# Half-size fetch and late split of three w_out row blocks, an earlier fetch of the second token tile, and other yields in the last head

## The chip, the cores and the metric

The kernel runs on one core of one Trainium2 chip. The metric is the device time of one execution in microseconds (us), the median of several runs. Before the change it is 2442.86 us (three runs, 2440.97 to 2443.92).

## The reference

One layer of a hybrid diffusion backbone over 2048 latent tokens of width 1024, with a context prefix of 256 tokens. Cut to what matters here:

```python
h = modulate(rmsnorm(x, norm_mix[l]), sh1, sc1)
o, _, _ = token_mixers(h @ w_in[l], ...)      # gated recurrence (4 heads) and spatial gating (4 heads)
x = x + g1 * (o @ w_out[l])                   # output projection, gated residual
h2 = modulate(rmsnorm(x, norm_ffn[l]), sh2, sc2)
x = x + g2 * conv_ffn(h2, w_up[l], conv_w[l], conv_b[l], w_down[l], rows)
return rmsnorm(x, norm_final)
```

Everything is float32. `w_out` has 1024 rows (eight blocks of 128, called k = 0 to 7) and 1024 columns (two halves of 512, called n = 0 and 1).

## The kernel before, in words

**Arithmetic.** A large product is made from three fp32r matmuls of 128x512 (`mm3`): each operand is split in a high part, made by a cast on ScalarE (ACT), and a low part, made by a subtraction, here on VectorE (DVE). The helper `split` (L133 and L134) issues both. The product is hi·hi + hi·lo + lo·hi.

**Stages.** The first stage (up to about 973 us of the profile) does the input projections (`pj`), the recurrence heads (`hg`, `deferred`) and the spatial gating heads (`sgu`). Its results go to DRAM as `oT`, one array for each half of the tokens. The second stage multiplies `oT` by `w_out`: 16 token tiles of 128 tokens, for each of them two column halves times eight row blocks times three matmuls, so 48 matmuls into a PSUM tile `dn`. The third stage is the up projection (tiles `Ah`, `Al`, results `ux`, `uz`) with the convolution, the fourth the down projection (`thl`, `mhl`).

**Order of the work.** The projections of the first stage run through `run_banks`, and between their matmuls two queues of side work are stepped: `hg_q` (heads) and `bg_q` (weights). A step is a Python generator that yields a number: it is the time in the program's own count of TensorE work that must pass before the next step is issued. `drain()` steps a queue to its end without regard to these numbers; `gates_done()` issues all pending output gates at once. A scheduler then orders the instructions of each engine; those wrapped in `pin` keep their program order. All DMAs are issued from one queue, that of SyncE (SP), in order: a DMA that must wait holds up those behind it.

**w_out.** `w_out_ops` (about 375 to 538 us) loads each of the 16 pieces (128 rows, 512 columns), multiplies it by the gate, splits it in `hi` and `lo` and stores both halves (512 KB) to `wo_d`. Blocks k = 0 to 2 are fetched back during the last recurrence head (`wo_early`, L916).

**The border.** Ahead of the last four projection banks (`wo_hook`, `seq[len(seq) - 4]`) `open_wo` runs: `hg_q.drain()`, `gates_done()`, `bg_q.drain()`, and then it closes the heads' SBUF pool and opens the pool `pw` in its place. Its generator `load` issues the fetch of the first token tile (`raw<-oT`, L1138) and ten fetches of 512 KB (`wo<-wo_d`, L1144: k = 3 to 7, for n = 0, then for n = 1), and after a yield of 17.0 splits the first tile into `o`. After the first stage's end the second stage's loop issues the fetch of the second token tile (`raw<-oT`, L1316, into a tile of the next pool), then the fetch of the residual rows (`raw<-in_x_dram`, L1326); at the head of iteration t the tile t+1 is split by `split_o`. The last two spatial gating products are made by GpSimd (POOL, L685) and stored by L686 (`oT<-nt`), on the same SP queue. The result of a tile is read by DVE (L1357) and squared by ACT (L1359).

**Placement.** Tiles with `align_bytes=AL` start at a multiple of 512 bytes in their partition; the others start wherever the packer puts them. Of the fp32r matmul operands the four of the heads' column sums (`kh`, `kl`, `knh`, `knl`) and `ones_r` have no such request; the others have.

Of the kernel before, what the change touches and what calls it, by code (L numbers as in the profile page):

```python
# [9 lines left out]
F32 = mybir.dt.float32  # L10
F32R = mybir.dt.float32r
# [7 lines left out]
P = 128  # L19
D = 1024  # L20
NK = D // P
# [5 lines left out]
NH = 4  # L27
# [4 lines left out]
EPS = 1e-6  # L32
LV = [1, 2, 4, 8, 16, 32, 64]
AL = 512

# [46 lines left out]
def tile_trunk(ctx, tc, x, c, cx, c_ctx, w_ada, b_ada, norm_mix, norm_ffn, w_in, hg_norm, sgu_g, sgu_b,  # L84
               w_sp, b_sp, w_out, w_up, conv_w, conv_b, w_down, norm_final, masks, out):
    nc = tc.nc
    V, S, G, T = nc.vector, nc.scalar, nc.gpsimd, Tensor(nc.tensor)
    ld = nc.sync.dma_start
    st = nc.sync.dma_start
    pin = tc.keep_in_program_order  # L90
# [25 lines left out]
    oT_d = [dr.tile([P, NK, TH], F32, name=f"oT{hh}") for hh in range(2)]  # L116
# [14 lines left out]
    def split(hi, lo, raw, eng=None, keep=lambda i: i):  # L131

        keep(S.copy(hi, raw))  # L133
        (eng or G).tensor_sub(lo, raw, hi.bitcast(F32))  # L134
# [48 lines left out]
    hg_q, bg_q = Pump(), Pump()  # L183
# [7 lines left out]
    with es1:  # L191
# [536 lines left out]
        def gate_later(hh, h, g0, on, r, sg):  # L728
            at = {"key": (hh, h), "to": (hh, h, g0, on, sg), "r": r}
            gates.append(at)  # L730
            hg_q.later(lambda: o_scale(at), 4.0)
            hg_q.later(lambda: gate_now(at), 7.5)

        def o_scale(at):
            r, on = at.pop("r", None), at["to"][3]
# [4 lines left out]
        def gate_now(at):  # L740
            if at in gates:
                o_scale(at)
                gates.remove(at)
                o_gate(*at["to"])
# [46 lines left out]
        def hg(hh, h, F, K, qs, vt, sgt):  # L791
# [90 lines left out]
            else:  # L882
# [1 line left out]
                st(dh_d[h], bs_[:, :NCH, :].rearrange("p c t -> p (c t)"))  # L884
                st(qb_d[h], Q[:, 0, :])
                st(sg_d[h], sgt)
            yield 7.0 if hh == 1 else 4.0
            on = []
            for g in range(0, NCH, 4):
                po = bank("mi")  # L890
# [31 lines left out]
        def deferred(h):  # L922

            Qb = ph.tile([P, 2, TH], F32, tag="Q", name="Qb", align_bytes=AL)[:, 0, :]
            sgt = ph.tile([P, NCH + 1, P], F32, tag="fs", name="sgb")[:, :NCH, :].rearrange("p c t -> p (c t)")
            op = ph.tile([P, TH], F32, tag="S", name="op")
            bs_ = ph.tile([P, NCH + 1, P], F32, tag="bst", name="bs2")
            ld(bs_[:, :NCH, :], dh_d[h].rearrange("p (c t) -> p c t", t=P))
            ld(Qb, qb_d[h])
            ld(op, op_d[h])  # L930
            ld(sgt, sg_d[h])
            yield 5.0
            chain(bs_, True, hb[h], lambda i: tb0[h][:, i:i + 1])
            yield 4.0
            on = []
            for g in range(0, NCH, 4):
                po = bank("mi")
                for i in range(4):
                    T.matmul(po[:, i * P:(i + 1) * P], Qb[:, (g + i) * P:(g + i + 1) * P], bs_[:, g + i + 1, :],
                             start=True, stop=True)  # L940
                sl = slice(g * P, g * P + 512)
                if g == 0:
                    gates_done()
                on.append(o_tile())
                V.tensor_add(on[-1], po, op[:, sl])
                on[-1] = on[-1], o_norm(on[-1])
                yield 1.0
            for g in range(2):
                gate_later(0, h, g * 512, *on[g], sgt)
# [32 lines left out]
        def w_out_ops():  # L982

            for n in range(2):
                cl = slice(n * 512, n * 512 + 512)
                g = pm.tile([P, 512], F32, tag="acc", name="g1")
                ld(g, g_d[0:1, cl].broadcast_to([P, 512]))
                for k in range(NK):
                    raw = raw_tile().rearrange("p (a c) -> p a c", a=2)
                    hi, w = raw[:, 0, :], raw[:, 1, :]  # L990
                    ld(w, w_out[k * P:(k + 1) * P, cl])
                    yield 8.0
                    V.tensor_mul(w, w, g)
                    split(hi.bitcast(F32R), w.bitcast(F32R), w, V)
                    st(wo_d[:, k, :, cl], raw)
                    yield 1.5

        def w_down_ops():
# [128 lines left out]
        def open_wo():  # L1127
            hg_q.drain()
            gates_done()
            bg_q.drain()  # L1130
            esh.close()
            pw = esw.enter_context(tc.tile_pool(name="pw", bufs=1, side="right", reuse_waits="tile"))
            first_o.append(lambda: pw.tile([P, 2, NK, P], F32R, tag="o", name="o", align_bytes=AL))
            early = len(wo)

            def load():
                raw = raw_tile().rearrange("p (k c) -> p k c", c=P)
                ld(raw, oT_d[0][:, :, 0:P])  # L1138
                for k in range(early, NK):
                    wo.append(pw.tile([P, 2, D], F32R, name=f"wo{k}", align_bytes=AL))  # L1140
                for n in range(2):
                    sl = slice(n * 512, n * 512 + 512)
                    for k in range(early, NK):
                        ld(wo[k][:, :, sl].bitcast(F32), wo_d[:, k, :, sl])  # L1144
                yield 17.0
                o = first_o[0]()
                split(o[:, 0], o[:, 1], raw, V, pin)
                first_o.append(o)
                yield 0.0
            bg_q.add(load())  # L1150
# [9 lines left out]
        run_banks(seq)  # L1160
        bg_q.drain()
        hg_q.flush()

# [26 lines left out]
    def dbank():  # L1192
        return ps2.tile([P, 2, 512], F32, tag="dn", name="dn", bufs=2)

    def a_tiles():
        return tuple(px.tile([P, 4, P], F32R, tag=w, name=w, bufs=4, align_bytes=AL) for w in ("Ah", "Al"))

    def v_tile():
        return px.tile([P, TH + GW], F32, tag="cv", name="cv", bufs=3)
# [73 lines left out]
    with tc.tile_pool(name="po", bufs=1, reuse_waits="tile") as po:  # L1273
        def second_norm(hh, g0, xs, ss, bank_, first, step):

            r = rstd(px, ss, 2, 1.0 / D)
            for i in range(2):
                scaled.append(V.tensor_scalar(out=xs[i], in0=xs[i], scalar1=r[:, i:i + 1], scalar2=None, op0=ALU.mult))
            yield first
            cl = slice(g0 // 2 * P, g0 // 2 * P + P)  # L1280
            for k in range(4):
                pt = bank_()
                for kk in range(2):
                    for i in range(2):
                        o = kk * 256 + i * P
                        T.transpose(pt[:, o:o + P], xs[i][:, (k + 4 * kk) * P:(k + 4 * kk + 1) * P], ident)
                yf = c_tile()
                fl = yf.bitcast(F32)
                for kk, dims in ((0, [[7 * P, 2], [1, P]]), (1, [[4 * P, 2], [1, P]])):
                    kq = k + 4 * kk  # L1290
                    pin(S.activation(view(fl, kk * P, dims),
                                     pt[:, kk * 256:kk * 256 + 256].rearrange("p (i c) -> p i c", c=P),
                                     AF.Identity, bias=s2[:, kq:kq + 1], scale=a2[:, kq:kq + 1]))
                pin(V.tensor_sub(fl[:, 3:5, :], view(fl, 7 * P, [[-2 * P, 2], [1, P]]), view(fl, 0, [[7 * P, 2], [1, P]])))
                V.tensor_sub(fl[:, 2, :], fl[:, 5, :], fl[:, 3, :])
                V.tensor_sub(fl[:, 6, :], fl[:, 1, :], fl[:, 2, :])
                hi = px.tile([P, 7, P], F32R, tag="yst", name="yst", bufs=2, align_bytes=AL)
                a = b = 0
                if hh == 0:
                    a, b = NR, NR - 1  # L1300
                    S.copy(xah[:, :, k, cl], fl[:, :a, :])
                    V.tensor_sub(xal[:, :, k, cl], fl[:, :b, :], xah[:, :b, k, cl].bitcast(F32))
                    V.tensor_sub(yf[:, b:a, :], fl[:, b:a, :], xah[:, b:a, k, cl].bitcast(F32))
                split(hi[:, a:, :], yf[:, a:7, :], fl[:, a:7, :], V)
                st(yd[hh][:, 0, a:, k, cl], hi[:, a:, :].bitcast(F32))
                st(yd[hh][:, 1, b:, k, cl], fl[:, b:7, :])
                yield step
# [5 lines left out]
        def fetch_o(t):  # L1313
            hh, g = tiles[t]
            raw = raw_tile2(2 * (t % 2 == 0)).rearrange("p a b -> p (a b)").rearrange("p (k c) -> p k c", c=P)
            ld(raw, oT_d[hh][:, :, g * P:(g + 1) * P])  # L1316
            return raw

        def split_o(t, raw):
            o = po.tile([P, 2, NK, P], F32R, tag="o", name="o", align_bytes=AL) if t % 2 else first_o[0]()  # L1320
            split(o[:, 0], o[:, 1], raw, V, pin)
            return o

# [2 lines left out]
            ld(xt.rearrange("p a b -> p (a b)"), x[t * P:(t + 1) * P, :])  # L1326
            return xt.rearrange("p a b -> p (a b)")

        raw_o = {1: fetch_o(1)}
        xts = {0: fetch_x(0)}  # L1330
        ops = {0: first_o[1]}
        xs = []
        for t, (hh, g) in enumerate(tiles):
            if g % 2 == 0:
# [231 lines left out]
    for n, (u, i) in enumerate(prods):  # L1566
# [18 lines left out]
        if n == 11:  # L1585
            bg_q.drain()
        if n == 12:
            edges = px.tile([P, 7, P], F32R, tag="yst", name="edges", bufs=2, align_bytes=AL).bitcast(F32)
            edges = edges[:, :4, :].rearrange("p f (w c) -> p f w c", w=2)
        with tc.issue_after(scaled[-1].ins) if n < 8 else nullcontext():  # L1590
            after(u, i, p)
# [271 lines left out]
```

## Time and profile before

| | |
|---|---|
| median of the runs | 2442.86 us |
| lowest and highest run | 2440.97 and 2443.92 us |
| the profiled execution | 2440.39 us |
| its span, first to last instruction | 2438.6 us |
| granted TensorE clock, mean | 0.996 |
| DVE busy | 1656.9 us (68%) |
| ACT busy | 1043.2 us (43%) |
| POOL busy | 867.8 us (36%) |
| DMA, mean over the span | 163 GB/s |

In the rows of the profile PE is TensorE's matmul, PEld its weight load. A row of the timeline gives start, duration, engine, line, operation, output<-inputs, count, and in brackets the idle time of the engine before it with what ended it. A row of the windows gives the stretch, its length, the busy time (number of instructions) of the engine, then the granted clock, the busy share of the DMA engines and the GB/s that they moved. A row of the waits gives who waited for what, the sum in us, how often, and the longest.

### The profile page before, as it was taken

The numbers are of one execution on the slowest core, as the hardware profiler recorded it, in microseconds if no ns is written. First come the engines' busy times: TensorE is split into PE (matmuls) and PEld (weight loads), VectorE is DVE, ScalarE is ACT, GpSimd is POOL, SyncE is SP. The second block draws the span as 40 slices with busy tenths as digits, with TensorE's granted clock in tenths as the row PEclk, the third lists the DMA queues.
The fourth block names the chain that finished last, engine by engine and source line by source line (L and its number), as shares of the span: only waits on it lengthen the run. The fifth ranks groups of instructions, "written<-read, shape, count | busy, mean of one in ns | idle before, by whom it ended". The sixth has DMA issues, their size and how long they took to land.

```text
span 2438.6 us, 32286 instructions
## 1 busy us (share of the span) xinstructions
PE 2402.0 (99%) x11711; PEld 1995.0 (82%) x11711; DVE 1656.9 (68%) x2253; ACT 1043.2 (43%) x1802; POOL 867.8 (36%) x788
## 2 busy tenths in 40 slices
PE   8999999999999999999999999999999999999998
PEld 5887887888888888788888888888888887888887
DVE  5757795765786785465596666639866772776875
ACT  3654344444444443354554444434445442332343
POOL 0021110210121122000688778787888870000002
PEclk9999999999999999999999999999999999999999
DMA  8365445463355234668922322562222238934755
GB/s 302 117 206 169 148 143 168 153 234 111 114 195 173 88 103 160 223 208 264 303 80 90 96 81 91 179 235 97 86 94 85 88 112 336 324 121 147 229 152 198
DMA packets 305581, 396.43 MB, mean 163 GB/s; under 512 B 32633, under 2 KB 215681, under 8 KB 302349
## 3 DMA queue, kind: packets, MB, share of 16 engines
q1 hardware_dynamic: 302132, 393.61, 48.6%
q8 instruction: 92, 1.51, 0.3%
q10 hardware_dynamic: 3289, 0.76, 0.1%
q14 instruction: 68, 0.56, 0.1%
HBM read 285.18 MB, written 109.13 MB: 162 GB/s over the span
## 4 chain that ended last, share of the span: by engine, by line
PE 54%; issue 2%; DMA 1%; DVE 1%; POOL 1%; ACT 1%; SPq 0%; POOLq 0%; ACTq 0%; DVEq 0%
PE dn L65 20%; PE ux L65 19%; PE uz L65 14%; PE pj L65 0%; POOL ra L1722 0%; DMA raw<-in_x_dram 0%; POOL rr L1723 0%; PE ux L69 0%; DMA raw<-in_w_up_dram 0%; DMA yf<-yd 0%; PE uz L69 0%; DVE dn L1433 0%; DMA yd<-fl 0%; POOL Al L134 0%; DVE cv L1357 0%
## 5 line engine op out<-in xcount | busy, mean ns | idle before, releaser
L1433 DVE SCALAR_TENSOR_TENSOR dn<-gp,taps,dn 128x1024 f32<-128x1024 f32 x352 | 448.2, 1284 | 97.5 <-ACT dn L1430 93.1
L65 PE MATMUL dn<-thl,mhl 128*128 128x512 f32 x1680 | 381.5, 389 | 1.2 <-ACT thl L133 1.2
L65 PEld LDWEIGHTS dn<-thl,mhl 128*128 128x128 f32 x1680 | 315.0, 188 | 67.7 <-ACT thl L133 2.1
L134 POOL TENSOR_TENSOR Al<-raw,Ah 128x512 fp32r<-128x512 f32 x264 | 341.7, 1311 | 65.8 <-ACT Ah L133 41.5
L65 PE MATMUL pj<-xh,whi 128*128 128x512 f32 x896 | 362.3, 405 | 0.3 <-ACT whi L133 0.3
L65 PE MATMUL pj<-xh,wlo 128*128 128x512 f32 x896 | 351.1, 392 | 1.2 <-DVE wlo L134 1.2
L65 PE MATMUL pj<-xl,whi 128*128 128x512 f32 x896 | 351.7, 393 | 0.0
L133 ACT CAST Ah<-raw 128x512 fp32r<-128x512 f32 x264 | 162.9, 620 | 238.9 <-PE ux L65 133.1
L65 PE MATMUL ux<-xah,Ah 128*128 128x512 f32 x528 | 205.7, 390 | 0.3 <-ACT keep L1497 0.3
L65 PEld LDWEIGHTS pj<-xh,wlo 128*128 128x128 f32 x896 | 168.3, 188 | 37.5 <-DVE wlo L134 2.1
L65 PEld LDWEIGHTS pj<-xh,whi 128*128 128x128 f32 x896 | 168.7, 188 | 34.2 <-issue 3.5
L65 PEld LDWEIGHTS pj<-xl,whi 128*128 128x128 f32 x896 | 168.9, 189 | 30.0 <-DVE xl L253 0.2
L65 PE MATMUL dn<-wo,o 128*128 128x512 f32 x768 | 184.4, 396 | 2.6 <-ACT o L133 2.1
L65 PE MATMUL uz<-yf,Ah 128*128 128x512 f32 x704 | 174.0, 389 | 0.0
L65 PEld LDWEIGHTS dn<-wo,o 128*128 128x128 f32 x768 | 143.0, 189 | 32.8 <-ACT o L133 2.5
L591 POOL TENSOR_TENSOR K<-K,tot 128x512 f32<-128x512 f32 x40 | 62.9, 1572 | 299.9 <-DVE tot L521 154.6
L65 PE MATMUL ux<-yf,Ah 128*128 128x512 f32 x528 | 155.4, 389 | 0.0
L65 PEld LDWEIGHTS uz<-yf,Ah 128*128 128x128 f32 x704 | 132.1, 188 | 27.4
L65 PE MATMUL ux<-xah,Al 128*128 128x512 f32 x528 | 141.8, 390 | 1.0 <-POOL Al L134 0.9
L65 PE MATMUL ux<-xal,Ah 128*128 128x512 f32 x352 | 137.0, 389 | 0.0
L1722 POOL TENSOR_SCALAR ra<-ss 128x1 f32<-128x1 f32 x8 | 5.3, 662 | 360.4 <-ACT jk L1714 360.4
L134 DVE TENSOR_TENSOR wlo<-raw,whi 128x1024 fp32r<-128x1024 f32 x68 | 84.1, 1236 | 68.3 <-ACT whi L133 67.3
(341 smaller groups left out, 4452.7 us busy)
## 6 DMA issues: line engine op xcount, KB each, us to landing
raw<-in_w_up_dram SPq DMA_DIRECT2D x88, 512.0 KB, 3.6
mr<-m SPq DMA_DIRECT2D x85, 512.0 KB, 5.5
raw<-in_w_in_dram SPq DMA_DIRECT2D x68, 512.0 KB, 4.0
sT<-wd SPq DMA_DIRECT2D x88, 256.0 KB, 5.8
raw<-in_w_ada_dram SPq DMA_DIRECT2D x32, 512.0 KB, 4.6
yf<-yd SPq DMA_DIRECT2D x14, 1024.0 KB, 10.4
m<-cv SPq DMA_DIRECT2D x22, 544.0 KB, 2.7
raw<-in_w_down_dram SPq DMA_DIRECT2D x22, 512.0 KB, 4.0
```

Source lines behind the costliest of these rows:

```text
L65: return self.engine.matmul(out, lhsT, rhs, **kw)
L133: keep(S.copy(hi, raw))
L134: (eng or G).tensor_sub(lo, raw, hi.bitcast(F32))
L591: e.tensor_mul(view(K2, row * W + o, src), view(K, o, src), view(tot, t0, [[4, n], [ts, 2], [0, B]]))
L1433: V.scalar_tensor_tensor(out=cr, in0=gt[:, t // 3:t // 3 + RH, t % 3:t % 3 + GW], scalar=taps[:, t * NF + f:t * NF + f + 1], in1=cr, op0=A ...
L1722: G.tensor_scalar(out=a, in0=ss, scalar1=plus, scalar2=None, op0=ALU.add)
```

## The change

- `w_out_ops`: for k = 5, 6, 7 the scaled piece is stored without being split (256 KB in place of 512 KB).
- `load`: these three blocks are fetched with 256 KB for each half, into the place of the low part; behind all fetches of `w_out` the second token tile is fetched into a tile `raw1` of the pool `pw`, which the second stage takes in place of its own fetch.
- At the end of the first stage, behind `hg_q.flush()`, the six pieces are split: six casts on ACT (pinned) and six subtractions on DVE.
- Three yields or delays of the last recurrence head (h = 3): 7.0 becomes 8.5 (`hg`, second half of the tokens), 4.0 becomes 4.8 (`deferred`), 7.5 becomes 8.7 (`gate_later`, first half of the tokens).
- `align_bytes=AL` is taken from `o` (both places), `wo` for k >= 3, `Ah`, `Al`, `yst` and `edges`.
- One `xbank()` and one `dbank()` are asked for and not used, ahead of the second stage, so that `ux` is placed ahead of `dn` in PSUM and the first `dn` in use is the second of its two places.

```diff
+LATE = (5, 6, 7)
...
-            hg_q.later(lambda: gate_now(at), 7.5)
+            hg_q.later(lambda: gate_now(at), 8.7 if (hh, h) == (0, NH - 1) else 7.5)
...
-            yield 7.0 if hh == 1 else 4.0
+            yield 8.5 if (hh, h) == (1, NH - 1) else 7.0 if hh == 1 else 4.0
...
-            yield 4.0
+            yield 4.8 if h == NH - 1 else 4.0
...
                     V.tensor_mul(w, w, g)
-                    split(hi.bitcast(F32R), w.bitcast(F32R), w, V)
-                    st(wo_d[:, k, :, cl], raw)
+                    if k in LATE:
+                        st(wo_d[:, k, 0, cl], w)
+                    else:
+                        split(hi.bitcast(F32R), w.bitcast(F32R), w, V)
+                        st(wo_d[:, k, :, cl], raw)
...
-            first_o.append(lambda: pw.tile([P, 2, NK, P], F32R, tag="o", name="o", align_bytes=AL))
+            first_o.append(lambda: pw.tile([P, 2, NK, P], F32R, tag="o", name="o"))
...
                 for k in range(early, NK):
-                    wo.append(pw.tile([P, 2, D], F32R, name=f"wo{k}", align_bytes=AL))
+                    wo.append(pw.tile([P, 2, D], F32R, name=f"wo{k}"))
                 for n in range(2):
                     sl = slice(n * 512, n * 512 + 512)
                     for k in range(early, NK):
-                        ld(wo[k][:, :, sl].bitcast(F32), wo_d[:, k, :, sl])
+                        if k in LATE:
+                            ld(wo[k][:, 1, sl].bitcast(F32), wo_d[:, k, 0, sl])
+                        else:
+                            ld(wo[k][:, :, sl].bitcast(F32), wo_d[:, k, :, sl])
+                raw1 = pw.tile([P, NK, P], F32, name="raw1")
+                ld(raw1, oT_d[0][:, :, P:2 * P])
+                first_o.append(raw1)
                 yield 17.0
...
         hg_q.flush()
+        for n in range(2):
+            sl = slice(n * 512, n * 512 + 512)
+            for k in LATE:
+                t = wo[k][:, :, sl]
+                split(t[:, 0], t[:, 1], t[:, 1].bitcast(F32), V, pin)
...
+    for first in (xbank, dbank):
+        first()
+
     def a_tiles():
-        return tuple(px.tile([P, 4, P], F32R, tag=w, name=w, bufs=4, align_bytes=AL) for w in ("Ah", "Al"))
+        return tuple(px.tile([P, 4, P], F32R, tag=w, name=w, bufs=4) for w in ("Ah", "Al"))
...
-        raw_o = {1: fetch_o(1)}
+        raw_o = {1: first_o[1]}
         xts = {0: fetch_x(0)}
-        ops = {0: first_o[1]}
+        ops = {0: first_o[2]}
```

More of the change, by code (lines that the diff above doesn't have):

```diff
@@ L1296, in second_norm @@
                 V.tensor_sub(fl[:, 6, :], fl[:, 1, :], fl[:, 2, :])
-                hi = px.tile([P, 7, P], F32R, tag="yst", name="yst", bufs=2, align_bytes=AL)
+                hi = px.tile([P, 7, P], F32R, tag="yst", name="yst", bufs=2)
                 a = b = 0
@@ L1319, in split_o @@
         def split_o(t, raw):
-            o = po.tile([P, 2, NK, P], F32R, tag="o", name="o", align_bytes=AL) if t % 2 else first_o[0]()
+            o = po.tile([P, 2, NK, P], F32R, tag="o", name="o") if t % 2 else first_o[0]()
             split(o[:, 0], o[:, 1], raw, V, pin)
@@ L1587, in tile_trunk @@
         if n == 12:
-            edges = px.tile([P, 7, P], F32R, tag="yst", name="edges", bufs=2, align_bytes=AL).bitcast(F32)
+            edges = px.tile([P, 7, P], F32R, tag="yst", name="edges", bufs=2).bitcast(F32)
             edges = edges[:, :4, :].rearrange("p f (w c) -> p f w c", w=2)
```

## The prediction

> **What bounds the kernel now.** I read the page first, then the waits of the matmul queue around the border between the first stage and the output projection, and then that border instruction by instruction. The page's row of busy times:
>
> ```profile
> PE 2402.0 (99%) x11711; PEld 1995.0 (82%) x11711; DVE 1656.9 (68%) x2253; ACT 1043.2 (43%) x1802; POOL 867.8 (36%) x788
> ```
>
> TensorE is busy for 99% of the span, so an edit that adds and removes no matmul can give at most its idle gaps and what a slow clock costs. The waits of PE from 925 to 1007 us:
>
> ```profile
> PE dn L65 <- ACT o L133: 2.1, 1, 2.1
> PE mi L69 <- DVE on L737: 1.5, 2, 1.0
> PE mi L65 <- DVE nt L709: 0.9, 1, 0.9
> PE mi L65 <- DVE bs__7975 L783: 0.6, 1, 0.6
> PE dn L65 <- DVE o L134: 0.5, 1, 0.5
> PE mi L65 <- issue: 0.5, 1, 0.5
> PE mi L65 <- DVE fs L777: 0.4, 1, 0.4
> ```
>
> There are two families: 2.6 us (2.1 + 0.5) in front of the second token tile's matmuls, and 3.0 us (1.5 + 0.6 + 0.5 + 0.4) in the last head (L709 belongs to the spatial gating, which the change leaves alone). The timeline of PE over the border, the whole-kernel chain's longest piece of plain matmuls, and the windows with the granted clock (fourth number) give the size of the first family:
>
> ```profile
> 973.57 11.15 PE L65 MATMUL dn<-wo,o 128*128 128x512 f32 x48
> 986.80 0.73 PE L65 MATMUL dn<-wo,o 128*128 128x512 f32 x2 [2.08 <-ACT o L133]
> 988.06 18.24 PE L65 MATMUL dn<-wo,o 128*128 128x512 f32 x73 [0.52 <-DVE o L134]
> 1006.14 0.73 PE L69 MATMUL ux<-ident,cv 128*128 128x128 f32 x4
> ```
> ```profile
> 2072.07 283.01 PE dn L65 x1247
> ```
> ```profile
> 957.00:969.00 12.00, 10.55 (x58) 1.00 0.51 158
> 969.00:976.00 7.00, 7.00 (x37) 1.00 1.06 404
> 976.00:985.00 9.00, 8.72 (x39) 1.00 1.07 386
> 987.70:991.00 3.30, 2.94 (x7) 0.50 0.39 109
> ```
>
> An undisturbed matmul takes 283.01 / 1247 = 0.227 us. From 973.57 to 1006.14 there are 48 + 2 + 73 = 123 of them: 27.9 us of work in 32.6 us. The border therefore loses **4.65 us**: 2.6 us of waiting, 1.65 us because the clock is at half from 987.7 to 991.0, and the rest in refilling after the two stops. This second cost is not in the list of waits; it comes with the first.
>
> Why the second tile is late is in the chain of waits of this window:
>
> ```profile
> 977.35 8.34 DMA raw<-in_x_dram
> 985.70 0.00 issue
> 985.70 1.05 ACT o L133
> ```
>
> and the order of the issues in SP's queue:
>
> ```profile
> 964.35 7.24 SPq L1144 DMA_DIRECT2D wo<-wo_d  x9
> 973.43 2.95 SPq L686 DMA_DIRECT2D oT<-nt  x2
> 976.48 0.83 SPq L1316 DMA_DIRECT2D raw<-oT  x1
> ```
>
> The tile's fetch (L1316) is issued only at 976.48, behind the two stores L686 that wait for GpSimd's products, and lands behind everything that is queued. The chain names the fetch of x, which the cast does not read: it is the landing seen last, and the tile's own data came at about the same time.
>
> **The change, part by part.** *Bytes and the early fetch.* The issues from 962.4 to 976.2, with their sizes:
>
> ```profile
> wo<-wo_d SPq DMA_DIRECT2D x10, 512.0 KB, 10.6
> raw<-oT SPq DMA_DIRECT2D x1, 512.0 KB
> oT<-nt SPq DMA_DIRECT2D x2, 256.0 KB
> oT<-ot SPq DMA_DIRECT2D x1, 256.0 KB, 2.1
> ```
> In MB, ahead of and with the second tile, today: 0.26 (last ot) + 0.52 + 10 x 0.524 + 2 x 0.26 + 0.52 = 7.07. By the windows 158 x 12 = 1.90 MB are moved by 969, 4.73 by 976, 7.07 at 976 + 2.34/0.386 = 982.1; ACT started at 985.7, so up to 3.6 us lie behind the last byte (the fetch of x shares the engines there). After: 0.26 + 0.52 + 4 x 0.524 + 6 x 0.262 = 4.45 with all of w_out, 4.98 with `raw1`. The same rates move 4.98 at 969 + 3.08/0.404 = 976.6; with the same 3.6 us it is usable at 980.2 at the latest. The cast (1.05, the chain) and subtraction (1.23, L134 below) end at 982.5. PE comes to that tile at 973.57 + 11.15 = 984.7, so there are **2.2 us to spare** and the whole 4.65 us go, the clock's part with them: waits of up to 1.0 us (L737 above, between 957 and 962) leave the clock at 1.00.
>
> *The six late splits.* The same two operations stand in the trace where they are removed (`w_out_ops`, on raw), and the border's own work around them is:
>
> ```profile
> L133 ACT CAST raw<-raw x16: 609/621/625, 376.1 to 534.9; 128x512 fp32r<-128x512 f32 x16
> L134 DVE TENSOR_TENSOR raw<-raw x16: 673/688/1767, 376.7 to 537.5; 128x512 fp32r<-128x512 f32 x16
> ```
> ```profile
> 972.96 0.60 ACT L690 ACTIVATE gu<-pj 128x512 f32<-128x512 f32 x1 [1.96 <-PE pj L65]
> ```
> ```profile
> 971.03 1.23 DVE L134 TENSOR_TENSOR o<-raw,o 128x1024 fp32r<-128x1024 f32 x1
> 973.85 0.75 DVE L717 SCALAR_TENSOR_TENSOR nt<-mi,vec,rh 128x512 f32<-128x512 f32 x1 [1.59 <-PE mi L65]
> ```
> ```profile
> 971.19 2.21 POOL L685 TENSOR_TENSOR nt<-nt,gu 128x512 f32<-128x512 f32 x1 [2.19 <-DVE nt L717]
> 974.74 1.29 POOL L685 TENSOR_TENSOR nt<-nt,gu 128x512 f32<-128x512 f32 x1 [1.33 <-issue]
> ```
>
> Six casts are 3.7 us of ACT, behind the gelu that ends at 973.56; six subtractions 4.1 us of DVE, behind L717 that ends at 974.60. Block 5 of n = 0 has landed by 969 + (2.09 - 1.90)/0.404 + 3.6 = 973.1; its cast is done at 974.2, its low part at 975.3, and PE wants them after 15 matmuls, at 977.0. The third piece has its low part at 976.7 and is wanted at 978.3. The last of n = 1 lands by 978.9 (4.45 MB), is split by 980.2 and wanted at 983.8. So their cover is the first tile's own 11 us of matmuls, and on PE they cost nothing; without that cover the first would cost 1.3 us. ACT and DVE then take the second tile's split, whose 2.2 us to spare hold. What they save at 376 to 538 us (as much again, on engines that are not the limit there) I put at nothing; the bound above is 0.7 us, one subtraction.
>
> *The wider steps.* These I take for idle. `open_wo` drains the head queue ahead of the last four banks, and the trace shows that the last head is in that drain:
>
> ```profile
> 932.07 3.73 PE L65 MATMUL mi<-vt,kt 128*128 128x128 f32 x32
> 935.64 0.39 PE L65 MATMUL mi<-vt,sc 128*128 128x128 f32 x2
> ```
>
> Between the state products and the outputs stand the yields 1.0 and 7.0, and no projection matmul lies between them: the second row follows the first at once. Neither of the first two yields is kept, the gates are forced by `gates_done()`, and the new numbers are as little used. So the 3.0 us of the last head stay, and these three edits cost and give 0 (bounds: a gain of 3.0 if all were honoured; a loss of the 3.5 by which the steps are widened in sum, less those 3.0, 0.5).
>
> *Placement and PSUM.* `Ah`, `Al`, `o` and `wo` lose their alignment. The nearest rows are fp32r operands without the request (`kh`, and `ones_r` as weights) beside the aligned ones:
>
> ```profile
> L65 PEld LDWEIGHTS sc<-kh,ones_r x16: 186/188/192, 222.7 to 874.8; 128*128 128x128 f32 x16
> L65 PE MATMUL sc<-kh,ones_r x16: 389/394/503, 222.9 to 875.1; 128*128 128x512 f32 x16
> ```
> ```profile
> L65 PEld LDWEIGHTS dn<-wo,o x768: 186/188/333, 973.5 to 1166.9; 128*128 128x128 f32 x192
> L65 PE MATMUL dn<-wo,o x768: 387/389/794, 973.6 to 1167.2; 128*128 128x512 f32 x192
> ```
>
> Weight loads are equal (188), matmuls 394 against 389 in the median, 389 against 387 at the least, and those 16 stand singly between other work. I take 0; the bounds are 0 and 5 ns on 3,696 (44 units x 7 products x 12) + 768 matmuls, 22 us. The PSUM order costs nothing: the new first `dn` lies on banks of `sc` and `pj`, whose last reader is at latest the gelu that ends at 973.56, where PE begins anyway.
>
> *The sum.* 2440.39 of the profiled execution - 4.65 = 2435.7. That execution is 2.5 us under the median of the runs, so off the median it is 2442.86 - 4.65 = **2438.2 us**, 0.19% less.
>
> A rule against this: the Trainium skill (SBUF — State Buffer, section "SBUF: two separate sides") says that DVE with two SBUF inputs and GpSimd take a shared port by exclusive lock, the loser being blocked for the whole instruction. The trace agrees: L685 took 2.21 us beside DVE's subtraction at 971.03 and 1.29 alone. By it the second L685 may have to wait for some of the six subtractions, and the sum would be that of rival 1; by the row at 974.74, which starts no later than they do, it stays at 2438.2.
>
> **The rivals.** *1, the wait comes back in part.* The product L685 at 974.74 now runs beside the subtractions. If it ends 4.1 us later, behind all six, its store is issued at 980.1 and landed 2.1 us later (the row of ot), at 982.2; the second tile's `o` lies in a pool opened over that product's place, so its cast would start there, the low part end at 984.5: just in time. With 1 to 2 us more a wait of that size returns, up to 1.0 us without the clock's dip, at 2.1 with it (1.65 more). For it: L685 took 2.21 us beside a subtraction and 1.29 alone. Against it: POOL starts at 974.74, as the first subtraction does, and 4 us is three times its own length. Time: 2442.86 - 4.65 + 1 = 2439.2, up to 2442.0 with 2.1 + 1.65.
> *2, the other side: placement.* If unaligned operands slow the stream of matmuls, 1.04 ns on each of 4,464 takes back the 4.65 us, and from 2.1 ns on the kernel is slower by 0.2%. At 5 ns it is 2442.86 - 4.65 + 22 = 2460. For it: the 394. Against it: the equal weight loads and the least of 389.
> *3, the wider steps are used* and take the head's waits away: 2442.86 - 4.65 - 3.0 = 2435.2. Against it: the drain above.
>
> **How the numbers follow.** Forecast 0.58, rival 1 0.18, rival 2 0.14, rival 3 0.10. The forecast's own range is 2436.7 to 2439.7, the spread of the three runs around it. The range for 8 in 10 goes from rival 3's 2435.2, rounded to 2435.0, to 2443.0, which takes in all of rival 1 and rival 2 up to the time before; rival 2 beyond that is left out. About 0.2% (4.9 us) is what a measurement of this kernel can tell from no change; the forecast of 4.65 lies at that bound, so of its 0.58 I count 0.34 as faster and 0.24 as within. With rival 3 and rounding, faster is 0.45; rival 1 gives the rest of within, 0.40; slower is 0.15, rival 2.
>
> **What would show it.** Right: L1316's first fetch gone and a second `raw<-oT` behind the `wo` fetches by 972; six casts on ACT from 973.5 and six subtractions; no wait of `dn` on `o` after the first 48 matmuls, clock 1.00 from 985 to 991, and 123 matmuls in 28 us. The last head's waits (L737, L783, L777) are still there with the same rows around them, and 24 of `ux` take 5.44 us as before. Wrong: a wait of `dn` on ACT or DVE `wo` inside the first tile, one on `o` after it, matmuls of `ux` or `dn` spaced by more than 0.227, or those head waits gone.

## The result, and the profile after

The changed kernel takes **2445.78 us** in the median (22 runs, 2443.14 to 2449.31); the kernel before, run beside it, takes 2439.40 us (22 runs, 2435.37 to 2443.92). The ratio is 1.0026, with a 95% interval of 1.0020 to 1.0032: it is slower by 0.26%, and the forecast of 2438.2 us and its range up to 2443.0 are both missed. The profiled execution took 2448.66 us, with a span of 2446.9 us.

Both halves of the story are in the profile. First the border. The waits of the matmul queue in the changed kernel, from 925 to 1010 us:

```profile
PE mi L70 <- DVE on L738: 1.4, 2, 1.0
PE dn L66 <- DVE nt L718: 0.9, 1, 0.9
PE mi L66 <- DVE nt L710: 0.9, 1, 0.9
PE mi L66 <- DVE bs__7963 L784: 0.6, 1, 0.6
PE mi L66 <- issue: 0.5, 1, 0.5
PE mi L66 <- DVE fs L778: 0.4, 1, 0.4
```

The two waits on `o` (2.1 and 0.5) are gone. The head's four are still there, within 0.1 us of their old sizes (1.4, 0.6, 0.5, 0.4). One row is new: the first `dn` waits 0.9 us for L718. The timeline of PE at the border, and a window over the place where the clock had been at half:

```profile
973.43 1.05 PE L66 MATMUL mi<-wsT,nt 128*128 128x128 f32 x8
975.42 28.62 PE L66 MATMUL dn<-wo,o 128*128 128x512 f32 x123 [0.94 <-DVE nt L718]
1003.88 0.69 PE L70 MATMUL ux<-ident,cv 128*128 128x128 f32 x4
```
```profile
985.00:991.00 6.00, 6.00 (x28) 1.00 0.62 191
```

All 123 matmuls run in one piece at clock 1.00, from 975.42 to 1003.88: 28.46 us in place of 32.57. Yet the span is 8.3 us longer. Where they went shows in the page's groups, the kernel before first and the changed one behind it (mean ns of one at the right of the busy time):

```profile
L65 PE MATMUL ux<-xah,Ah 128*128 128x512 f32 x528 | 205.7, 390 | 0.3 <-ACT keep L1497 0.3
L65 PE MATMUL uz<-yf,Ah 128*128 128x512 f32 x704 | 174.0, 389 | 0.0
```
```profile
PE 2410.9 (99%) x11711; PEld 1994.4 (82%) x11711; DVE 1660.0 (68%) x2253; ACT 1044.2 (43%) x1802; POOL 865.1 (35%) x788
...
L66 PE MATMUL ux<-xah,Ah 128*128 128x512 f32 x528 | 207.0, 392 | 0.3 <-ACT keep L1515 0.3
L66 PE MATMUL uz<-yf,Ah 128*128 128x512 f32 x704 | 175.8, 392 | 0.0
```

PE is busy 8.9 us longer with the same 11,711 matmuls, and the up projection, which no edit of the change touches except in where its operands lie, has 392 ns for one matmul in place of 389. The duration of one (392) is longer than the distance to the next, since they overlap; the sharper view counts how many fit into the same 700 us in the middle of the up projection, with no idle time in either kernel:

```profile
1250.00:1950.00 700.00, 700.00 (x3090) 1.00 0.33 110
```
```profile
1250.00:1950.00 700.00, 700.00 (x3060) 1.00 0.33 110
```

The kernel before does 3090 (226.5 ns each), the changed one 3060 (228.8). The granted clock is 1.00 in both and the DMA share is equal. From first to last matmul of each stage, worked out from the starts in the two traces:

| us | before | after | difference |
|---|---|---|---|
| start of the output projection | 973.57 | 975.42 | +1.85 |
| output projection | 193.59 | 191.56 | -2.03 |
| up projection | 842.11 | 850.21 | +8.10 |
| down projection | 420.99 | 421.38 | +0.39 |

They add up to the 8.3 us of the span. The first row is the least firm: over the profiled executions of this study that start lies between 968.9 and 975.4 us, whatever the kernel, which is why times below are compared by medians and causes by stages.

### The profile page after: what moved, and what is told of

Read it like the earlier page. It is cut to its first block, busy times and chain, and to the rows that moved or that the text cites. A ratio compares the mean times of both kernels' runs of the same rounds, so it can differ in the third digit from the quotient of the medians.

```text
span 2446.9 us, 32289 instructions
## 1 busy us (share of the span) xinstructions
PE 2410.9 (99%) x11711; PEld 1994.4 (82%) x11711; DVE 1660.0 (68%) x2253; ACT 1044.2 (43%) x1802; POOL 865.1 (35%) x788
## 5 line engine op out<-in xcount | busy, mean ns | idle before, releaser
L135 POOL TENSOR_TENSOR Al<-raw,Ah 128x512 fp32r<-128x512 f32 x264 | 342.1, 1312 | 76.1 <-ACT Ah L134 44.2
```

## The experiments

Two theories stood against each other for the 8.1 us: that the operands' place in SBUF slows the stream of matmuls, or that something else in the change does (the PSUM order, the transfers, the first stage's other layout). Four more questions followed: which place counts, whether the fewer bytes or the earlier fetch took the border's wait away, what the PSUM order costs, and what is left when only the useful part stays. "Offset" below is the distance of a tile's start in its partition behind a multiple of 512 bytes; it is read from the program. Before the change it is 0 for `Ah`, `Al`, `yst`, `o`, `wo`, `xah`, `xal`, `yf`, `mhl` and `thl`. After it, `Ah`, `Al` and `yst` are at 192, `wo` for k >= 3 at 32, `o` at 32 for even token tiles and at 192 for odd ones; the rest stay at 0.

**1. The placement of the up projection alone, in the kernel before.**

```diff
-        return tuple(px.tile([P, 4, P], F32R, tag=w, name=w, bufs=4, align_bytes=AL) for w in ("Ah", "Al"))
+        return tuple(px.tile([P, 4, P], F32R, tag=w, name=w, bufs=4) for w in ("Ah", "Al"))
...
-                hi = px.tile([P, 7, P], F32R, tag="yst", name="yst", bufs=2, align_bytes=AL)
+                hi = px.tile([P, 7, P], F32R, tag="yst", name="yst", bufs=2)
...
-            edges = px.tile([P, 7, P], F32R, tag="yst", name="edges", bufs=2, align_bytes=AL).bitcast(F32)
+            edges = px.tile([P, 7, P], F32R, tag="yst", name="edges", bufs=2).bitcast(F32)
```

> The kernel before, with the alignment taken from Ah, Al and yst alone: Ah and Al then start 192 bytes past a multiple of 512, as in the changed kernel, and nothing else of the change is in it. Theory P (placement of the weights against the moving rows): the up projection's matmuls go from 226.7 to about 228.9 ns, 8 us more over the 3,696 of them, the border wait of 2.6 us stays, so about +8 us, ratio 1.003. Rival S (PSUM order, DMA traffic or the late splits slow the stage): the up projection keeps 226.7 ns and the time is that of before.

Measured: 2447.56 us against 2438.78, a ratio of 1.0031 (1.0021 to 1.0041). The up projection takes 849.93 us, the output projection keeps its 228.4 ns from one start to the next, and the same window reads:

```profile
1250.00:1950.00 700.00, 700.00 (x3060) 1.00 0.33 109
```

Nothing else of the change is in this kernel, and it is slower by as much as the up projection is longer (7.8 us in the stage, 8.8 in the medians with an interval of 5.1 to 10.0). The loss is the placement.

**2. The whole change, with the operands back on multiples of 512 bytes.** Two unused tiles move everything behind them; no `align_bytes` comes back.

```diff
+                pads.append(pw.tile([P, 8], F32, name="padw"))
...
+                if not padded:
+                    padded.append(px.tile([P, 80], F32, name="padx"))
+                    G.memset(padded[0][:, :1], 0.0)
                 hi = px.tile([P, 7, P], F32R, tag="yst", name="yst", bufs=2)
```

> The changed kernel with two pad tiles (320 bytes ahead of yst, 32 bytes behind o in pw), so that Ah, Al, yst, wo and both o start at a multiple of 512 bytes again, without any alignment asked for. Theory P: all matmuls back at 226.7 ns, the gain at the border stays: first 123 matmuls of the output projection in about 28 us, 4 us faster than before (ratio 0.998). Rival S: the up projection stays at 228.9 ns and the time is that of the changed kernel.

Measured: 2436.55 us, a ratio to the kernel before of 0.9990 (0.9981 to 0.9999). That is 2.2 us, not the 4 that were expected; experiments 4 and 5 say why. Window and border:

```profile
1250.00:1950.00 700.00, 700.00 (x3090) 1.00 0.33 110
```
```profile
975.33 28.15 PE L66 MATMUL dn<-wo,o 128*128 128x512 f32 x123 [0.94 <-DVE nt L718]
```

The 3090 are back, the up projection takes 842.13 us, and the output projection falls from 191.56 to 189.40 us, with 228.3 ns in place of 231.3 from start to start. So the placement cost 8.1 us in the one and 2.2 us in the other, and the border's gain stands without it.

**3. Which place? Two ladders and two shifts.** In the ladders, which also have the pads of experiment 2, each of the four buffers of `Ah` and `Al` is a tile of its own with 32 bytes behind it, so that `Ah0`, `Al0`, `Ah1`, ... `Al3` lie at 0, 32, 64, ... 224; in the second ladder 64 more words ahead put them at 256 to 480. What they meet (`xah`, `xal`, `yf`) stays at 0.

```diff
-        return tuple(px.tile([P, 4, P], F32R, tag=w, name=w, bufs=4) for w in ("Ah", "Al"))
+        j = count[0] % 4
+        count[0] += 1
+        out = []
+        for w in ("Ah", "Al"):
+            out.append(px.tile([P, 4, P], F32R, tag=f"{w}{j}", name=f"{w}{j}x"))
+            if count[0] <= 4:
+                padded.append(px.tile([P, 8], F32, name=f"pad{w}{j}"))
...
+                    padded.append(px.tile([P, 80], F32, name="padx"))
```

> The padded change with each of the four Ah and four Al tiles at a place of its own: Ah 0, 64, 128, 192 and Al 32, 96, 160, 224 bytes past a multiple of 512; moving rows (xah, xal, yf) at 0. Theory P: the products' time depends on the slot; 0 gives 226.7 ns a matmul, 192 gives 228.9, those at odd multiples of 32 as much or more. Rival S: no difference between the slots.

> The padded change with Ah at 256, 320, 384, 448 and Al at 288, 352, 416, 480 bytes past a multiple of 512, the moving rows at 0: the upper half of the ladder. Theory P1 in its plain form (any difference costs): all slots above 226.7 ns. Theory P3 (only the difference within 256 bytes counts): 256 is at 226.7 ns and the upper half repeats the lower one.

Measured (one run each): 2457.73 and 2455.19 us, and 861.85 and 861.84 us for the up projection. The groups of PE from 1250 to 1950 us, the low ladder first:

```profile
L66 PE MATMUL uz<-yf,Ah3x 128*128 128x512 f32 x226 | 56.5, 392 | 0.0
L66 PE MATMUL uz<-yf,Ah1x 128*128 128x512 f32 x200 | 50.6, 394 | 0.0
...
L66 PE MATMUL uz<-yf,Ah2x 128*128 128x512 f32 x88 | 22.2, 394 | 0.0
L66 PE MATMUL uz<-yf,Ah0x 128*128 128x512 f32 x64 | 15.9, 390 | 0.0
```
```profile
L66 PE MATMUL uz<-yf,Ah3x 128*128 128x512 f32 x224 | 55.9, 392 | 0.0
L66 PE MATMUL uz<-yf,Ah1x 128*128 128x512 f32 x200 | 50.6, 394 | 0.0
...
L66 PE MATMUL uz<-yf,Ah2x 128*128 128x512 f32 x88 | 22.2, 394 | 0.0
L66 PE MATMUL uz<-yf,Ah0x 128*128 128x512 f32 x64 | 15.9, 390 | 0.0
```

Same means, slot by slot, 256 bytes apart. From start to start, worked out from the two traces (ns):

| offset, low ladder | 0 | 32 | 64 | 96 | 128 | 160 | 192 | 224 |
|---|---|---|---|---|---|---|---|---|
| low | 227.9 | 231.3 | 232.5 | 230.9 | 232.3 | 232.9 | 229.4 | 232.9 |
| high (256 more) | 227.9 | 231.3 | 232.5 | 230.9 | 232.3 | 232.9 | 229.4 | 232.9 |

At 0 and at 256 the steady distance is 226 to 227; the mean of 227.9 has the passage from a slower neighbour in it. The 192 that the change happened to get is, behind 0, the cheapest of the eight: the ladders cost 19.7 us in the stage.

The next kernel gives the operands of the up projection an offset in common, 192 for all of them, and leaves `thl` at 0 in the down projection while `mhl`, which takes the place of `xal`, is at 192:

```diff
+    padb = pb.tile([P, 72], F32, name="padb")
...
-    xah = pb.tile([P, NR, 4, 512], F32R, tag="xah", name="xah", align_bytes=AL)
+    xah = pb.tile([P, NR, 4, 512], F32R, tag="xah", name="xah")
...
+                    padded.append(px.tile([P, 40], F32, name="padx"))
```

(`xal`, `yf`, `mhl` and `sT` lose their request in the same way.)

> The changed kernel with the moving rows of the up projection (xah, xal, yf) put 192 bytes past a multiple of 512 as well, the place of Ah and Al; mhl, which follows xal, goes to 192 too, while thl in the down projection stays at 0. Theory P1 (the difference of the two places counts): the up projection is back at 226.7 ns (8 us less than the changed kernel) and the down projection's 1,680 go from 226.7 to about 229 ns (about 4 us more). Theory P2 (each operand must itself lie at a multiple of 512): the up projection is at 228.9 ns or more, and the down projection slower too.

Measured: 2436.57 us (one run). Two windows, one in the up and one in the down projection; behind them the down projection of the kernel before:

```profile
1250.00:1950.00 700.00, 700.00 (x3090) 1.00 0.33 109
...
2100.00:2400.00 300.00, 300.00 (x1312) 1.00 0.57 185
```
```profile
2100.00:2400.00 300.00, 300.00 (x1325) 1.00 0.59 193
```

With all at 192 the up projection is at full pace (3090; 841.97 us), and the down projection, in which one operand is now at 192 and the other at 0, has lost pace (1312 for 1325; 228.9 ns for 226.7 from start to start; 424.58 us for 420.99). So an offset by itself costs nothing; the difference between the two operands of a matmul does.

The last of this group is the padded change of experiment 2 with 144 words in place of 80, which puts `Ah`, `Al`, `yst` and the odd tiles of `o` at 256 against partners at 0.

> The change whole, with pads that put Ah, Al, yst and the odd token tiles of o at 256 bytes behind a multiple of 512, everything that they meet at 0. If only the difference modulo 256 bytes counts: up projection 842 us, 226.75 ns from start to start, output projection 228.4 ns, and the time of the padded change, about 2435 us. If a difference of 256 costs what the unaligned kernel pays: 850 us or more and 2444 us or more.

Measured: 2436.04 us (one run); up projection 842.38 us, 226.77 ns; output projection 189.58 us, 228.2 ns.

```profile
1250.00:1950.00 700.00, 700.00 (x3090) 1.00 0.33 110
```

A difference of 256 is as good as none. What counts is the difference modulo 256 bytes.

The traces show the same in two places at which no experiment aimed. In the changed kernel's output projection `o` (the weights) and `wo` (the moving rows) of the row blocks k >= 3 differ by 0 in even token tiles and by 160 in odd ones: from start to start they take 228.6 and 234.2 ns, against 228.0 and 228.2 in experiment 2. The row blocks k < 3 are fewer and fit less evenly: 4.7 ns more in even tiles, where the table has 4.6 for 32, but 0.6 more in odd ones, where it has 2.7 for 192. And the down projection begins with 72 matmuls whose moving rows are `Ah` and `Al`, at 192 in the changed kernel, against `mhl` at 0. They take 18.07 us there and 17.67 before, which is all of the stage's 0.39 us, while the 1,680 of `thl` and `mhl` take 381.8 us in both. These 72 lose 5.5 ns each and not 2.2: here it is the rows that lie 192 further on, so weights minus rows is -192, which is 64 modulo 256, and the table has 5.8 ns for 64 (232.5 - 226.7). So the difference is to be taken with its sign.

**4. Fewer bytes or the earlier fetch?** The padded change (experiment 2) without one and without the other. First, all pieces at full size again:

```diff
-LATE = (5, 6, 7)
+LATE = ()
```

> The padded change with LATE empty: all of w_out split early, stored and fetched at full size, the second tile still fetched right behind it. Theory R1 (the place in SP's queue decides): no wait of dn on the second o, first 123 matmuls in 28 us. Theory R2 (the bytes are needed too): 1.57 MB more ahead of it are 3.9 us at 404 GB/s, against some 2 us to spare, so a wait of up to 2 us returns.

Measured: 2435.49 us (one run), and in the timeline of PE:

```profile
971.25 11.13 PE L66 MATMUL dn<-wo,o 128*128 128x512 f32 x48 [0.94 <-DVE nt L718]
982.70 0.73 PE L66 MATMUL dn<-wo,o 128*128 128x512 f32 x2 [0.33 <-ACT o L134]
983.96 16.89 PE L66 MATMUL dn<-wo,o 128*128 128x512 f32 x73 [0.53 <-DVE o L135]
```

Beside the kernel before this looks like a gain: waits of 0.33 and 0.53 us in place of 2.08 and 0.52, the clock at 1.00, 29.44 us for the 123 matmuls. But the kernel of experiment 1 has the border of the kernel before, untouched, and its profile reads:

```profile
970.50 11.15 PE L65 MATMUL dn<-wo,o 128*128 128x512 f32 x48
982.72 0.73 PE L65 MATMUL dn<-wo,o 128*128 128x512 f32 x2 [1.07 <-ACT o L133]
983.98 16.86 PE L65 MATMUL dn<-wo,o 128*128 128x512 f32 x73 [0.53 <-DVE o L134]
```

Here too the clock stays at 1.00, and the 123 take 30.18 us. So the same border lost 4.65 us in one execution and 2.3 in the other. With so much spread one profile of a shorter wait proves little, and part of it comes from the first `dn`, which starts 1.2 us later here than in those two (experiment 5). Second, half the bytes, but the fetch in its old place behind the first stage:

```diff
-                raw1 = pw.tile([P, NK, P], F32, name="raw1")
-                ld(raw1, oT_d[0][:, :, P:2 * P])
-                first_o.append(raw1)
...
-        raw_o = {1: first_o[1]}
+        raw_o = {1: fetch_o(1)}
```

> The padded change with the second tile fetched where it was before (behind GpSimd's two stores, into a tile of the next pool), the late splits and half sizes kept. Theory R1: issued at about 977 again, landing 3 to 5 us later with the queue now nearly empty, split by 984, so no wait or under 1 us, and no clock dip. Theory R3 (the early fetch is what matters): the wait of 2 us and the dip of the clock are back, first 123 matmuls in 31 us or more.

Measured: 2435.08 us (one run), no wait on `o`:

```profile
971.86 28.14 PE L66 MATMUL dn<-wo,o 128*128 128x512 f32 x123 [0.94 <-DVE nt L718]
```

The 123 take 27.97 us. A steadier measure than the wait is how long after the first stage's last `mi` the cast of the second tile starts, read from the starts in the traces (us):

| | last `mi` | cast | later by |
|---|---|---|---|
| kernel before | 972.76 | 985.70 | 12.9 |
| experiment 1, the same border | 969.69 | 981.62 | 11.9 |
| the early fetch alone | 969.26 | 981.60 | 12.3 |
| half the bytes alone | 969.87 | 979.12 | 9.3 |
| both (experiment 2) | 973.34 | 981.70 | 8.4 |

Half the bytes are enough by themselves and bring the cast some 3 us forward. The early fetch alone does not bring it forward; beside the half bytes it is not needed, and the other kernels that have both (8.2 to 9.6 us) show no gain from it.

**5. The PSUM order.** The padded change without the two unused calls:

```diff
-    for first in (xbank, dbank):
-        first()
```

> The padded change without the unused xbank and dbank, so that ux and dn lie in PSUM as before. Theory Q (the first dn now lies on a bank of mi, whose last reader is DVE's L718): the wait of 0.9 us of the first dn on nt goes, the first dn follows the last mi matmuls at 0.8 us as before instead of 2.0, 1.2 us less than the padded change; about 3 to 4 us faster than before. Rival: the wait is taken over by another reader and nothing changes.

Measured: 2433.71 us against 2437.07, a ratio of 0.9989 (0.9980 to 0.9998).

```profile
971.18 1.05 PE L66 MATMUL mi<-wsT,nt 128*128 128x128 f32 x8
971.99 28.15 PE L66 MATMUL dn<-wo,o 128*128 128x512 f32 x123
```

The wait on L718 is gone: the first `dn` starts 0.81 us behind the first `mi`, against 1.99 in the changed kernel (975.42 - 973.43). That is 1.2 us in every trace that has the two calls. In the times it can't be told: 0.9989 here and 0.9990 in experiment 2 have intervals that cover each other.

**6. What is left when only the useful part stays.** Half-size pieces and late splits, operands on multiples of 512, the old PSUM order, the old place of the fetch (experiments 2, 5 and the second of 4 together).

> The half-size pieces and their late splits alone: operands kept on multiples of 512 bytes by two pads, the old PSUM order, the second token tile fetched at its old place behind the first stage (the wider yields left in, which change no order). If the bytes alone take the border's wait away: no wait on o, 123 matmuls in 28.0 us, up projection 842 us with 226.75 ns from start to start, and the same time as with the pads and the old PSUM order, a ratio of 0.997 to 0.999. If the early fetch is needed beside the old PSUM order, where the first output matmul starts 1.2 us earlier: a wait on o of 0.3 to 1.3 us and 123 matmuls in 28.5 to 30 us.

Measured: 2435.00 us (11 runs) against 2438.34, a ratio of 0.9986 (0.9977 to 0.9995).

```profile
970.75 1.05 PE L66 MATMUL mi<-wsT,nt 128*128 128x128 f32 x8
971.56 28.15 PE L66 MATMUL dn<-wo,o 128*128 128x512 f32 x123
```

No wait, and 27.99 us for the 123. The second tile's low part ends at 981.93 and is wanted at 971.56 + 11.15 = 982.71: it holds, with 0.8 us to spare. This kernel and that of experiment 5 are faster than the kernel before by 0.1%, with intervals that end below 1, and so faster than the changed one; which of the two is the better the intervals don't tell.

## Why the prediction failed, step by step

**The step that failed is the placement.** It was put at 0 inside bounds of 0 and 5 ns; the truth is +2.2 ns on the 3,696 matmuls of the up projection (8.1 us) and +3 ns on the 768 of the output projection (2.2 us), 10.3 us in all and well inside the 22 us of the upper bound. Rival 2 is the case that came, and its arithmetic was right: it set the point from which the kernel is slower by 0.2% at 2.1 ns, and the measured mean over the 4,464 is 10.3 / 4,464 = 2.3 ns. It had a chance of 0.14.

Why the row that was chosen misled: `kh` with `ones_r` was taken as "operands without the request". In the program before, `ones_r` lies at offset 128 and `kh` at 384. They are 256 apart, the one distance other than 0 that cost nothing in experiment 3. Lack of a request is not a place; the addresses were there to be read, and with them that row would have counted for nothing. The median of 394 in it, which the prediction noted and took as a sign for rival 2, is then no sign of this effect: where two products on `ones_r` follow each other without a gap, the next starts 227 ns later (at 697.80 and 698.03 us). What lengthens the others, which stand singly, was not measured.

The equal weight loads did not speak against rival 2. They stay equal where the stream is slow, in the rows of the two pages (before, then after):

```profile
L65 PEld LDWEIGHTS uz<-yf,Ah 128*128 128x128 f32 x704 | 132.1, 188 | 27.4
```
```profile
L66 PEld LDWEIGHTS uz<-yf,Ah 128*128 128x128 f32 x704 | 132.1, 188 | 28.8
```

**The border: right in its mechanism, one execution's in its size.** The forecast gain was 4.65 us; between the profiles 32.57 us became 28.46, and 27.99 with the placement restored, a gain of 4.6. Behind the wait of 2.1 us the clock was at half, behind that of 1.1 in experiment 1 it was not. But the loss of 4.65 was read from one execution, and the untouched border of experiment 1 lost 2.3. In the medians the kernel of experiment 5 gains 3.4 us (0.5 to 4.9) and that of experiment 6 3.3 (1.2 to 5.6), which neither figure contradicts. Of its reasons, that fewer bytes bring the tile in time is shown (experiments 4 and 6); that the early fetch is part of it is not.

**The late splits** are hidden by the first tile's matmuls, as forecast. ACT and DVE in the changed kernel:

```profile
974.12 1.65 ACT L134 CAST wo<-wo 128x512 fp32r<-128x512 f32 x3
977.68 2.01 ACT L134 CAST wo<-wo 128x512 fp32r<-128x512 f32 x3 [1.91 <-DMA wo<-wo_d]
982.19 1.05 ACT L134 CAST o<-raw 128x1024 fp32r<-128x1024 f32 x1 [2.50 <-DMA oT<-nt]
```
```profile
972.01 2.25 DVE L135 TENSOR_TENSOR o<-raw,o 128x1024 fp32r<-128x1024 f32 x1 [0.26 <-ACT o L134]
974.52 0.75 DVE L718 SCALAR_TENSOR_TENSOR nt<-mi,vec,rh 128x512 f32<-128x512 f32 x1 [0.26 <-PE mi L66]
975.19 2.98 DVE L135 TENSOR_TENSOR wo<-wo 128x512 fp32r<-128x512 f32 x3
978.33 2.09 DVE L135 TENSOR_TENSOR wo<-wo 128x512 fp32r<-128x512 f32 x3 [0.16 <-ACT wo L134]
983.27 1.23 DVE L135 TENSOR_TENSOR o<-raw,o 128x1024 fp32r<-128x1024 f32 x1 [2.86 <-ACT o L134]
```

The second tile's cast starts at 982.19, 2 us behind the 980.2 that was forecast; the profile names the last store (`oT<-nt`) as what it waited for. Its low part is done at 984.5 and wanted at 975.42 + 11.15 = 986.6, so there are 2.1 us to spare, 1.2 of them because the first `dn` starts later. With the old PSUM order little is left of the 2.2 us that were forecast: 0.8 in experiment 6 and 0.1 in experiment 5 (low part done at 983.06, wanted at 983.14). That no wait came there is in part luck.

**Rival 1** did not come, though the cast starts at the 982.2 that it gives. POOL's last two products, and their stores in SP's queue:

```profile
971.89 1.29 POOL L686 TENSOR_TENSOR nt<-nt,gu 128x512 f32<-128x512 f32 x1 [2.19 <-DVE nt L718]
975.40 1.62 POOL L686 TENSOR_TENSOR nt<-nt,gu 128x512 f32<-128x512 f32 x1 [2.23 <-ACT wo L134]
```
```profile
973.74 3.62 SPq L687 DMA_DIRECT2D oT<-nt  x2
```

The second one starts beside the first of the six subtractions and takes 1.62 us, not 4.1 more; its store is issued by 977.36, and if the profile names the right wait, it was landed 4.8 us later, where rival 1 had reckoned 2.1. The subtraction of `o` that begins at 972.01, while the first product runs to 973.18, takes 2.25 us where it takes 1.23 alone: the two engines do hold each other up, about 1 us at a time, in the order in which they come. With that the trace agrees with the exclusive lock of the Trainium skill (SBUF — State Buffer, section "SBUF: two separate sides"). The lock changes hands between two subtractions, so the product is not held behind all six.

**The PSUM order** was put at nothing, because the new first `dn` was thought to lie on banks of `sc` and `pj`. The program has, in the first stage, `mi` in banks 0 to 2, `sc` in 3 and 4 and `pj` in 5 to 7; `dn` moved from banks 0 to 3 to banks 2 to 5, its first one from 0 and 1 to 2 and 3, and the last `mi` is in bank 2. The step named the wrong last reader: not the gelu, but L718, which reads `mi` and ends at 975.27, 0.15 us ahead of the first `dn`. The term is a wait of 0.9 us and a start 1.2 us later.

**The wider steps** are idle, as forecast: the head's waits are the same rows, and with the three old numbers put back in the changed program every engine gets the same instructions in the same order. Rival 3 falls.

**The base.** The three runs shown lay 3.5 us above the 2439.40 of all 22 runs, of which they are part. Against that base the forecast of -4.65 us would have been 2434.8, and the miss larger. Experiment 6, which has the border without the placement and the PSUM order, gives 2435.00 beside 2438.34 for the kernel before. The terms set to 0 decided.

Added up over the profiled stages: output projection -4.2 (experiment 2 against before) + 2.2, up projection + 8.1, down projection + 0.4, wait at the start + 1.2 of the 1.85, which makes 7.7 us; the medians say 6.4, with an interval of 4.9 to 7.8. The -4.2 is the least firm of these terms: against the output projection of experiment 1 (191.90 us, with the smaller loss at its border) it would be -2.5 and the sum 9.4, above that interval.

## What to carry to other kernels

An edit that moves buffers is an edit of every instruction that reads them: look up where each operand of the long, gap-free stages lands before and after, and weigh a nanosecond by the number of instructions (2.2 ns on 3,696 outweighed the whole gain at the border here). For fp32r matmuls like these keep the two SBUF operands of a product at the same distance behind a multiple of 256 bytes; a request for alignment is one way, a pad of some words another. When a "free" row is used as evidence that a property costs nothing, make sure that the row has the property. And a loss that was read from one profiled execution is one sample: a second profile of the same stretch, here that of experiment 1, shows how far it varies.

## What the runs showed of the hardware

- The pace of a stream of 128x512 fp32r matmuls depends on the difference, weights minus rows and modulo 256 bytes, between the starts of its two SBUF operands: 226.7 ns at 0 and 256, 229 to 233 ns at the other multiples of 32, 192 (228.9 when all differ by it) being the cheapest of them. The granted clock is 1.00 throughout and the weight loads keep their 187 to 189 ns, in the ladders too. The Trainium skill (SBUF — State Buffer, section "Operand start alignment") gives an operand's start as a matter of legality and says that its measurements timed nothing; these did.
- At 192 the distances are not evenly longer but repeat in threes, about 226, 229 and 232 ns. The same page, section "SBUF: two separate sides", has TensorE wait on no other engine. The runs don't contradict that: the difference that matters is one between TensorE's own two operands, which would fit weights and moving rows that meet in reading. That mechanism was not shown: no run takes the weight loads or the rows away, and only offsets that are multiples of 32 bytes were tried.
- What stays open: the start of the output projection varies by 6.5 us between profiled executions of nearly the same first stage, the loss at the untouched border by 2.3 us between the two that have it, and a difference of 192 costs the row blocks k < 3 of the output projection less than it costs the up projection.
